# Low halves of an MLP's down weights: an adding DMA onto the negated high half, in place of a VectorE subtraction

## The chip, the cores and the metric

One core of a Trainium2 chip. The metric is the device time of one execution of the whole program in microseconds (us); lower is better. The kernel computes a forward pass on 512 tokens of width 1024, in float32.

## What is computed

The program runs a first block (two attentions, a memory cross-attention, a SwiGLU MLP) and then two layers of a second block, layer 0 (an mLSTM mixer) and layer 1 (latent attention). Both layers end in the MLP that the change touches, with w1 of 1024 x 4096 and w2 of 4096 x 1024:

```python
def sqrelu_mlp(h, w1, w2):
    return jnp.square(jax.nn.relu(h @ w1)) @ w2
...
    for l in range(DEPTH_2):
        ada = cond @ ada_w[l] + ada_b[l]
        sh1, sc1, g1, sh2, sc2, g2 = jnp.split(ada, 6, axis=-1)
...
        h = modulate(rmsnorm(x, norm_g[l, 2]), sh2, sc2)
        y = sqrelu_mlp(h, mlp_w1[l], mlp_w2[l])
        x = x + g2[:, None, :] * rmsnorm(y, norm_g[l, 3])
```

The products keep float32 accuracy: each operand is cut into a high part `hi`, the value rounded to the chip's short float32 form (fp32r), and a low part `lo = value - hi`. A product is then three matmuls: hi by hi, hi by lo, and lo by hi.

## The kernel before

**Weights.** Every weight matrix passes through one mechanism. `weights` (L410) declares *takes*: a take is a piece of a matrix of 512 KB, for a down matrix two k-tiles of 128 rows by 512 columns. `pump` loads the raw take with a DMA on SP's queue (L421) into one of four `raw` buffers, and calls `split` (L286), which allots one tile of the `s8` pool (14 buffers) for hi and lo together and appends the work in pieces. `plain` is a piece: ScalarE (ACT) copies the raw 128x512 to hi (L307), VectorE (DVE) subtracts hi from raw into lo (L308, where `f` is DVE here). In the stretches between two stages that the kernel calls quiet, every second hi is written by GpSimd (POOL, L304) in place of ACT. How many split takes may be held at once is the cap: 4, 3, 4, 4 and 4 in the five blocks of the MLP here (`caps`), and 7 while the last block's down products run. A raw buffer is free again when its last piece is done.

**The MLP.** `mlp` (L1322 on) goes over the 32 k-tiles of the hidden layer in blocks of 6, 8, 6, 6 and 6. For each block `up` makes the hidden tiles, squared ReLU and its split included, and the down products of that block add into eight accumulators. Block 0 comes from plain pairs of products (`relu_pairs`); blocks 1 to 4 from a Winograd form (`wino`): the product of quarters of w1 and h is made from seven smaller products, its matmuls of 256 columns are on L508, its combinations of PSUM results on DVE (L522 to L532), its weight sums in `split7` (ACT L341, DVE L342, L345, L361). The sums of h's quarters that it needs are made once by POOL (L480). Per layer the down products take 6, 8, 6, 6 and 6 takes, 32 in all; each feeds 24 matmuls of 512 columns (hi by hi on L445, hi by lo on L446, lo by hi on L447).

**Beside it.** During layer 0's MLP a background generator makes the rows `ada` of layer 1 and the shared keys: raw blocks of ada_w come in over SP's queue into `araw`, DVE multiplies and adds them up (L852), splits the sum (ACT L633, DVE L634), PE sums over the partitions (L869), DVE adds the bias row (L886). POOL issues the small DMAs around it (L201 for norm_g, ada_b and the store to `arow`; L585 reads rows back) and clears a tile for each row (L843). Layer 1's MLP has none of this beside it.

**Order.** The program is one stream per engine. A scheduler that simulates a timeline (`schedule_with_timeline_sim`) sets each engine's order when the kernel is built, so an edit can move instructions that it does not name. On each engine the instructions then run in order, and one that waits holds back all behind it. The raw loads are on SP's queue, the `ada` stores, row loads and small loads on POOL's.

Of the kernel before, what the change touches and what calls it, by code (L numbers as in the profile page):

```python
# [10 lines left out]
F32 = mybir.dt.float32  # L11
# [3 lines left out]
AF = mybir.ActivationFunctionType  # L15
ALU = mybir.AluOpType
# [5 lines left out]
S = 512  # L22
# [116 lines left out]
class Net:  # L139
# [64 lines left out]
    def pump(self):  # L204

        if self.dry:
            return
        more = True
        while more:
            more = False  # L210
            if self.n_load < len(self.specs):
                i = self.n_load
                kk, cc, loaders = self.specs[i][:3]
                if self.raw_live + len(loaders) <= BUF["raw"]:
                    self.raws[i] = [self.t("raw", [P, kk, cc], F32, BUF["raw"]) for _ in loaders]
                    for f in self.before.pop(i, ()):
                        f()
                    for loader, raw in zip(loaders, self.raws[i]):
                        loader(self, raw)
                    self.n_load += 1  # L220
                    self.raw_live += len(loaders)
                    more = True
            i, p = self.n_ready
            if i < self.n_load and self.w_live < self.wcap:
                kk, cc, loaders, gain = self.specs[i]
                if len(loaders) == 1:
                    self.ready[i, 0] = self.split(i, self.raws.pop(i)[0], kk, cc, gain)
                    self.n_ready = i + 1, 0
                else:
                    self.ready[i, p] = self.split7(i, p, self.raws[i])  # L230
                    self.n_ready = (i, p + 1) if p < 3 else (i + 1, 0)
                    if p == 3:
                        self.raws.pop(i)
                self.w_live += 1
                if not self.quiet and not BUF["sp"]:
                    while self.pieces:
                        _, last, f = self.pieces.pop(0)
                        f()
                        self.raw_live -= last
                more = True  # L240
# [13 lines left out]
            self.credit -= sp  # L254
            self.piece()

    def take(self, kk, cc, loader, gain=None):


        if self.dry:  # L260
            self.specs.append((kk, cc, loader, gain))
        self.n_take += 1
        return self.n_take - 1

# [18 lines left out]
            self.w_live -= 1  # L283
            self.pump()

    def split(self, c, src, kk, cc, gain):  # L286

        A, V = self.nc.scalar, self.nc.vector
        both = self.big([P, 2, kk, cc], F32R)
        hi, lo = both[:, 0], both[:, 1]  # L290
# [27 lines left out]
            V.scalar_tensor_tensor(out=lo[:, i, :], in0=src[:, i, :], scalar=g, in1=hi[:, i, :].bitcast(F32),  # L318
                                   op0=ALU.mult, op1=ALU.subtract)

        if gain is not None:
            todo = [lambda i=i: scaled(i) for i in range(kk)]
        else:
            m = min(cc, 512)
            todo = [lambda i=i, j=j: plain(slice(i, min(i + n, kk)), slice(j, j + m))
                    for i in range(0, kk, n) for j in range(0, cc, m)]
# [83 lines left out]
            self.step_bg()  # L410
        return self.gcols[name]

    def weights(self, w, k0, nk, c0, cn, view=None, gain=None, into=None):
        g = into or Group(self)
        kk = max(1, min(nk, 1024 // cn))
        for k in range(k0, k0 + nk, kk):
            n = min(kk, k0 + nk - k)

            def loader(net, raw, k=k, n=n):
                if view is None:  # L420
                    net.nc.sync.dma_start(out=raw, in_=w[k * P:(k + n) * P, c0:c0 + cn].rearrange(  # L421
                        "(k p) c -> p k c", p=P))
                else:
                    for i in range(n):
                        dst, src = view(raw[:, i, :], w[(k + i) * P:(k + i + 1) * P, :])
                        net.nc.sync.dma_start(out=dst, in_=src)

            g.add(self.take(n, cn, (loader,), gain and (gain, k)), n)
        return g

    def step_bg(self, n=1):
# [887 lines left out]
    def mlp(self, blocks, up, w_down, g, nxt, first, ready=None, caps=None):  # L1319
# [4 lines left out]
        for b, nb in enumerate(blocks):  # L1324
# [25 lines left out]

            if last:
                self.cap(BUF["lc"], True)
                wgs = [self.weights(w_down, k0, nb, c * S, S) for c in range(2)]

                def y_of(t):
                    ms = part(t, 0, product(t, wgs[0])) + part(t, 1, product(t, wgs[1]))
                    return acc[t], ms

                self.boundary(y_of, nxt, first)
            else:  # L1360
                for c in range(2):
                    wg = self.weights(w_down, k0, nb, c * S, S)
                    pss = [self.bank() for _ in range(NT)]
                    for k in range(0, nb, 2):
                        for t in range(NT):
                            self.run(self.prod(pss[t], [(hid.k(i, tt(t)), wg.k[i]) for i in (k, k + 1)],
                                               (lambda i: wg.used(k + i)) if t == NT - 1 else None,
                                               first=k == 0, last=k == nb - 2))
                    for t in range(NT):
                        part(t, c, pss[t])  # L1370
# [589 lines left out]
```

## Time and profile before

| | |
|---|---|
| median of 3 runs | 2034.83 us (2032.62 to 2037.33) |
| the profiled execution | 2033.3 us, span 2031.5 us, mean granted clock 0.982 |
| PE busy | 1941.8 us, 96 % of the span |
| DVE busy | 1396.7 us, 69 % |
| ACT busy | 1025.0 us, 50 % |
| POOL busy | 331.7 us, 16 %, 615 instructions |
| SP's DMA queue | 232.15 MB, 37.0 % of 16 engines |
| POOL's DMA queue | 11.10 MB, 1.9 % |
| chain that ended last | PE 69 %, DVE 14 %, issue 6 %, DMA 5 %, ACT 4 %, POOL 2 % |

The profiled execution took 2033.3 us by the clock of the runs, 1.8 us more than the span between its first and last instruction. Shares are means over stages that differ; the two MLPs in question lie at about 1100 to 1434 us (layer 0) and 1697 to 2024 us (layer 1). PE is TensorE, whose clock the chip throttles: 1.00 in the clock column is full speed.

### The profile page before, as it was taken

Reading aid. Unit: us, or ns where it says so; the run is one execution under the profiler, and the core shown is the slowest. Engines: PE = TensorE matmul, PEld = TensorE weight load, DVE = VectorE, ACT = ScalarE, POOL = GpSimd, SP = SyncE. Lnnn points to the kernel's source line nnn. Section 1 sums busy time; section 2 is a strip of 40 time slices with the busy share of each in tenths; the row PEclk is TensorE's granted clock in tenths of the full one; section 3 lists DMA queues with packets and bytes.
Section 4 is the critical chain, followed back from the end, with each engine's and each line's share of the span. In section 5 each row is a group of like instructions: output and inputs, shape, how many; then the busy total and the mean of one; then the engine's idle time right before and its main releaser. Section 6 shows DMA issues by size and latency. Waiting matters only on the chain.

```text
span 2031.5 us, 29708 instructions
## 1 busy us (share of the span) xinstructions
PE 1941.8 (96%) x10684; PEld 1665.1 (82%) x10684; DVE 1396.7 (69%) x2659; ACT 1025.0 (50%) x2283; POOL 331.7 (16%) x615
## 2 busy tenths in 40 slices
PE   8999998999999999999998899999979999999998
PEld 5888987778888888778888788798767978989987
DVE  5756645756576576757767897889758656657666
ACT  7767874545244233347534363454545644545444
POOL 1321113003000000421126100000330034000001
PEclk9999999999999999999999999999989999999999
DMA  7322341433465465244333355555342203233322
GB/s 219 89 79 76 118 129 61 137 104 103 157 202 159 137 203 142 83 142 129 120 104 113 117 163 156 183 167 159 102 134 89 73 12 103 83 104 115 103 74 83
DMA packets 191667, 245.14 MB, mean 121 GB/s; under 512 B 20059, under 2 KB 119488, under 8 KB 191520
## 3 DMA queue, kind: packets, MB, share of 16 engines
q1 hardware_dynamic: 185264, 232.15, 37.0%
q0 software_dynamic: 6256, 11.10, 1.9%
q8 instruction: 84, 1.38, 0.3%
q14 instruction: 63, 0.52, 0.1%
HBM read 241.00 MB, written 2.20 MB: 120 GB/s over the span
## 4 chain that ended last, share of the span: by engine, by line
PE 69%; DVE 14%; issue 6%; DMA 5%; ACT 4%; POOL 2%; DVEq 0%; POOLq 0%; ACTq 0%
PE ps L447 18%; PE ps L446 18%; PE ps L445 18%; PE ps L508 7%; DMA araw<-in_ada_w 3%; DVE u L852 2%; DVE s L308 2%; DVE s L318 2%; PE ps L1011 1%; DVE s L634 1%; DVE s L342 1%; DVE x L654 1%; ACT junk L579 1%; PE ps L1793 1%; PE ps L1822 1%
## 5 line engine op out<-in xcount | busy, mean ns | idle before, releaser
L445 PE MATMUL ps<-s,s 128*128 128x512 f32 (+4 forms) x2260 | 857.8, 383 | 8.4 <-ACT s L633 4.8
L446 PE MATMUL ps<-s,s 128*128 128x512 f32 (+4 forms) x2260 | 850.5, 377 | 12.2 <-DVE s L634 11.9
L447 PE MATMUL ps<-s,s 128*128 128x512 f32 (+4 forms) x2260 | 845.2, 377 | 4.7 <-DVE s L634 4.6
L446 PEld LDWEIGHTS ps<-s,s 128*128 128x128 f32 (+1 forms) x2260 | 431.7, 191 | 90.0 <-DVE s L634 13.7
L447 PEld LDWEIGHTS ps<-s,s 128*128 128x128 f32 (+1 forms) x2260 | 430.2, 190 | 86.7 <-DVE s L634 7.4
L445 PEld LDWEIGHTS ps<-s,s 128*128 128x128 f32 (+1 forms) x2260 | 429.7, 191 | 84.9 <-ACT s L633 7.5
L508 PE MATMUL ps<-s,s 128*128 128x256 f32 x2184 | 265.3, 282 | 10.0 <-DVE u L524 6.9
L508 PEld LDWEIGHTS ps<-s,s 128*128 128x128 f32 x2184 | 262.8, 189 | 13.8 <-issue 5.9
L852 DVE SCALAR_TENSOR_TENSOR u<-araw,cond,u 128x512 f32<-128x512 f32 x224 | 177.2, 791 | 108.6 <-DMA araw<-in_ada_w 87.2
L308 DVE TENSOR_TENSOR s<-raw,s 128x512 fp32r<-128x512 f32 x277 | 193.3, 736 | 42.5 <-ACT s L307 37.0
L307 ACT ACTIVATE s<-raw 128x512 fp32r<-128x512 f32 x255 | 144.9, 622 | 152.8 <-PE ps L447 96.4
L317 ACT ACTIVATE s<-raw,cols_all 128x256 fp32r<-128x256 f32 (+1 forms) x283 | 134.2, 547 | 47.5 <-issue 22.1
L318 DVE SCALAR_TENSOR_TENSOR s<-raw,cols_all,s 128x256 fp32r<-128x256 f32 (+1 forms) x305 | 150.5, 546 | 8.7 <-ACT s L317 7.3
L201 POOL DMA_DIRECT2D arow<-u x30 | 14.7, 492 | 629.6 <-DVE u L886 378.9
L568 POOL TENSOR_SCALAR sm<-sm 128x1 f32<-128x1 f32 x74 | 20.5, 277 | 558.9 <-ACT junk L579 556.1
L634 DVE TENSOR_TENSOR s<-ps,s 128x512 fp32r<-128x512 f32 (+3 forms) x124 | 75.2, 619 | 40.6 <-ACT s L633 39.7
L341 ACT ACTIVATE s<-raw 128x512 fp32r<-128x512 f32 x104 | 62.6, 621 | 67.9 <-PE ps L447 32.9
L634 DVE TENSOR_TENSOR s<-u,s 128x512 fp32r<-128x512 f32 x102 | 69.7, 686 | 39.4 <-ACT s L633 35.8
L633 ACT ACTIVATE s<-u 128x512 fp32r<-128x512 f32 x102 | 63.6, 625 | 64.0 <-DVE u L1403 49.3
L633 ACT ACTIVATE s<-ps 128x512 fp32r<-128x512 f32 (+3 forms) x124 | 65.2, 538 | 38.3 <-PE ps L626 16.1
L341 ACT ACTIVATE s<-u 128x512 fp32r<-128x512 f32 x78 | 48.7, 624 | 61.0 <-DVE u L345 31.6
L342 DVE TENSOR_TENSOR s<-raw,s 128x512 fp32r<-128x512 f32 x104 | 70.5, 682 | 11.0 <-ACT s L341 10.9
(264 smaller groups left out, 2211.7 us busy)
## 6 DMA issues: line engine op xcount, KB each, us to landing
raw<-in_mlp_w SPq DMA_DIRECT2D x128, 512.0 KB, 4.0
araw<-in_ada_w SPq DMA_DIRECT2D x192, 256.0 KB, 3.0
raw<-in_w_gate_up SPq DMA_DIRECT2D x44, 512.0 KB, 4.3
raw<-in_w_in SPq DMA_DIRECT2D x24, 512.0 KB, 4.6
raw<-in_a_w_in SPq DMA_DIRECT2D x24, 512.0 KB, 4.0
raw<-in_w_down SPq DMA_DIRECT2D x22, 512.0 KB, 4.1
raw<-in_w_mem_kv SPq DMA_DIRECT2D x16, 512.0 KB, 3.6
araw<-in_kv_ada_w SPq DMA_DIRECT2D x32, 256.0 KB, 3.1
```

The costliest lines, as they stand in the source:

```text
L307: A.activation(hi[:, sl, cl], src[:, sl, cl], AF.Copy)
L308: f.tensor_tensor(out=lo[:, sl, cl], in0=src[:, sl, cl], in1=hi[:, sl, cl].bitcast(F32), op=ALU.subtract)
L317: A.activation(hi[:, i, :], src[:, i, :], AF.Copy, scale=g)
L318: V.scalar_tensor_tensor(out=lo[:, i, :], in0=src[:, i, :], scalar=g, in1=hi[:, i, :].bitcast(F32), op0=ALU.mult, op1=ALU.subtract)
L341: A.activation(hi, x, AF.Copy)
L445: self.nc.tensor.matmul(ps, lhsT=ah, rhs=bh, start=first and i == 0, stop=False)
L446: self.nc.tensor.matmul(ps, lhsT=ah, rhs=bl, start=False, stop=False)
L447: self.nc.tensor.matmul(ps, lhsT=al, rhs=bh, start=False, stop=last and i == n - 1)
L508: nc.tensor.matmul(ps, lhsT=l[:, k, :], rhs=m[:, k, :], start=first and k == e == 0, stop=k == 3 and e == 2, skip_group_check=True)
L633: self.nc.scalar.activation(hi, x, AF.Copy)
L634: self.nc.vector.tensor_tensor(out=lo, in0=x, in1=hi.bitcast(F32), op=ALU.subtract)
L852: V.scalar_tensor_tensor(out=acc, in0=raws.pop(j - 2), scalar=vec[:, j - 2:j - 1], in1=acc, op0=ALU.mult, op1=ALU.add)
```

## The change

Takes can be marked `far`. The down takes of the squared-ReLU MLPs are (`caps` is set for these alone): 32 in each layer, 64 in all. For a far take, ACT writes hi as before, in two instructions, but within one piece; POOL then writes lo = -hi over the whole 128x1024, with a tensor_scalar (L326 of the changed kernel); and POOL issues a DMA that adds the raw take onto lo (L327), from SBUF to SBUF, 512 KB. So 128 subtractions leave DVE, 64 tensor_scalars and 64 DMAs come to POOL, and no far take's hi is made by POOL any more. The sums are the same. Lines behind the insertion stand 10 further down: L445, L446 and L447 become L455, L456 and L457, L508 becomes L518.

```diff
--- before.py
+++ after.py
@@ -222,9 +222,9 @@
                     more = True
             i, p = self.n_ready
             if i < self.n_load and self.w_live < self.wcap:
-                kk, cc, loaders, gain = self.specs[i]
+                kk, cc, loaders, gain, far = self.specs[i]
                 if len(loaders) == 1:
-                    self.ready[i, 0] = self.split(i, self.raws.pop(i)[0], kk, cc, gain)
+                    self.ready[i, 0] = self.split(i, self.raws.pop(i)[0], kk, cc, gain, far)
                     self.n_ready = i + 1, 0
                 else:
                     self.ready[i, p] = self.split7(i, p, self.raws[i])
@@ -254,11 +254,11 @@
             self.credit -= sp
             self.piece()
 
-    def take(self, kk, cc, loader, gain=None):
+    def take(self, kk, cc, loader, gain=None, far=False):
 
 
         if self.dry:
-            self.specs.append((kk, cc, loader, gain))
+            self.specs.append((kk, cc, loader, gain, far))
         self.n_take += 1
         return self.n_take - 1
 
@@ -283,7 +283,7 @@
             self.w_live -= 1
             self.pump()
 
-    def split(self, c, src, kk, cc, gain):
+    def split(self, c, src, kk, cc, gain, far=False):
 
         A, V = self.nc.scalar, self.nc.vector
         both = self.big([P, 2, kk, cc], F32R)
@@ -318,7 +318,17 @@
             V.scalar_tensor_tensor(out=lo[:, i, :], in0=src[:, i, :], scalar=g, in1=hi[:, i, :].bitcast(F32),
                                    op0=ALU.mult, op1=ALU.subtract)
 
-        if gain is not None:
+        def away():
+
+            G = self.nc.gpsimd
+            for i in range(0, kk, n):
+                A.activation(hi[:, i:i + n, :], src[:, i:i + n, :], AF.Copy)
+            G.tensor_scalar(out=lo, in0=hi.bitcast(F32), scalar1=-1.0, scalar2=1.0, op0=ALU.mult, op1=ALU.mult)
+            G.dma_start(out=lo, in_=src, accum_op=ALU.add)
+
+        if far:
+            todo = [away]
+        elif gain is not None:
             todo = [lambda i=i: scaled(i) for i in range(kk)]
         else:
             m = min(cc, 512)
@@ -410,7 +420,7 @@
             self.step_bg()
         return self.gcols[name]
 
-    def weights(self, w, k0, nk, c0, cn, view=None, gain=None, into=None):
+    def weights(self, w, k0, nk, c0, cn, view=None, gain=None, into=None, far=False):
         g = into or Group(self)
         kk = max(1, min(nk, 1024 // cn))
         for k in range(k0, k0 + nk, kk):
@@ -425,7 +435,7 @@
                         dst, src = view(raw[:, i, :], w[(k + i) * P:(k + i + 1) * P, :])
                         net.nc.sync.dma_start(out=dst, in_=src)
 
-            g.add(self.take(n, cn, (loader,), gain and (gain, k)), n)
+            g.add(self.take(n, cn, (loader,), gain and (gain, k), far), n)
         return g
 
     def step_bg(self, n=1):
@@ -1350,7 +1360,7 @@
 
             if last:
                 self.cap(BUF["lc"], True)
-                wgs = [self.weights(w_down, k0, nb, c * S, S) for c in range(2)]
+                wgs = [self.weights(w_down, k0, nb, c * S, S, far=caps is not None) for c in range(2)]
 
                 def y_of(t):
                     ms = part(t, 0, product(t, wgs[0])) + part(t, 1, product(t, wgs[1]))
@@ -1359,7 +1369,7 @@
                 self.boundary(y_of, nxt, first)
             else:
                 for c in range(2):
-                    wg = self.weights(w_down, k0, nb, c * S, S)
+                    wg = self.weights(w_down, k0, nb, c * S, S, far=caps is not None)
                     pss = [self.bank() for _ in range(NT)]
                     for k in range(0, nb, 2):
                         for t in range(NT):
```

**What moves.** On PE, at the start of layer 1's second block, nothing does. Here `s_3357` is the tile of the block's first down take, `s_3309` and `s_3310` hold the hidden tile's hi and lo. Before, from the last of the four L445 that open the block:

```order
L445 MATMUL ps_17758<-s_3357_17686,s_3309_17339 128x512
L508 MATMUL ps_17622<-s_3268_16975,s_3352_17651 128x256 [waits DVE_49]
L508 MATMUL ps_17622<-s_3268_16975,s_3352_17651 128x256 x9
L446 MATMUL ps_17755<-s_3357_17686,s_3309_17339 128x512 [waits DVE_49]
L447 MATMUL ps_17755<-s_3357_17686,s_3310_17340 128x512
L445 MATMUL ps_17755<-s_3357_17686,s_3309_17339 128x512 [waits Activation_49]
```

and with the change:

```order
L455 MATMUL ps_17758<-s_3357_17686,s_3309_17339 128x512
L518 MATMUL ps_17622<-s_3268_16975,s_3352_17651 128x256 [waits DVE_49]
L518 MATMUL ps_17622<-s_3268_16975,s_3352_17651 128x256 x9
L456 MATMUL ps_17755<-s_3357_17686,s_3309_17339 128x512 [waits DMASW1_49]
L457 MATMUL ps_17755<-s_3357_17686,s_3310_17340 128x512
L455 MATMUL ps_17755<-s_3357_17686,s_3309_17339 128x512 [waits Activation_49]
```

The matmuls stand in the same order, and the first one that reads lo waits for a DMA queue's semaphore in place of DVE's.

At the start of the third block of layer 1 PE's order is another (`s_3429` is the first down take, `s_3404` and `s_3405` hidden hi and lo; L508 rows are Winograd products of the next tiles). Before, again from the last of the four L445:

```order
L445 MATMUL ps_18437<-s_3429_18329,s_3404_18154 128x512
L446 MATMUL ps_18434<-s_3429_18329,s_3404_18154 128x512 [waits DVE_49]
L447 MATMUL ps_18434<-s_3429_18329,s_3405_18155 128x512
L445 MATMUL ps_18434<-s_3429_18329,s_3404_18154 128x512 [waits Activation_49]
L508 MATMUL ps_18297<-s_3184_16434,s_3418_18262 128x256 [waits Activation_49]
L508 MATMUL ps_18297<-s_3184_16434,s_3418_18262 128x256 x11
L446 MATMUL ps_18434<-s_3429_18329,s_3404_18154 128x512 [waits DVE_49]
L447 MATMUL ps_18434<-s_3429_18329,s_3405_18155 128x512
L446 MATMUL ps_18435<-s_3429_18329,s_3404_18154 128x512
L447 MATMUL ps_18435<-s_3429_18329,s_3405_18155 128x512
```

and with the change:

```order
L455 MATMUL ps_18437<-s_3429_18329,s_3404_18154 128x512
L518 MATMUL ps_18297<-s_3184_16434,s_3418_18262 128x256 [waits Activation_49]
L518 MATMUL ps_18297<-s_3184_16434,s_3418_18262 128x256
L518 MATMUL ps_18297<-s_3184_16434,s_3418_18262 128x256 [waits DVE_49]
L518 MATMUL ps_18297<-s_3184_16434,s_3418_18262 128x256 x9
L518 MATMUL ps_18298<-s_3232_16635,s_3418_18262 128x256 [waits DVE_49,Activation_49]
L518 MATMUL ps_18298<-s_3232_16635,s_3418_18262 128x256 x11
L518 MATMUL ps_18300<-s_3268_16975,s_3419_18281 128x256 [waits DVE_49]
L518 MATMUL ps_18300<-s_3268_16975,s_3419_18281 128x256 x11
L456 MATMUL ps_18434<-s_3429_18329,s_3404_18154 128x512 [waits DMASW1_49]
L457 MATMUL ps_18434<-s_3429_18329,s_3405_18155 128x512
```

The first hi by lo came right behind the four hi by hi; now 36 Winograd matmuls stand between them. The fourth and fifth blocks of layer 1 are ordered in this manner too.

On POOL, at the start of layer 0's MLP, before (`s_2070`, `s_2072`, `s_2074` are the first three down takes, `s_2106` the fourth; `u_2093` and on belong to the `ada` rows):

```order
L304 TENSOR_SCALAR s_2070_10684<-raw_10432 128x512 [waits DMAHW3_49,PE_49]
L304 TENSOR_SCALAR s_2072_10727<-raw_10507 128x512 [waits DMAHW4_49,PE_49]
L304 TENSOR_SCALAR s_2074_10746<-raw_10525 128x512 [waits DMAHW5_49,PE_49]
L585 DMA row_14375<-arow_4063 128x320 [waits DMASW1_49,DVE_49]
L201 DMA u_2093_10790<-in_kv_norm_g 1x16x32
L843 MEMSET u_2097_10836 128x512 [waits DMASW5_49]
L201 DMA u_2097_10836<-in_ada_b 1x16x32 [waits Pool_49]
L201 DMA arow_4063<-u_1934_9982 16x1x32 [waits DMASW2_49,DVE_49]
L381 DMA u_2094_10806<-arow_4063 8x128 [waits DMASW2_49]
```

and with the change:

```order
L326 TENSOR_SCALAR s_2070_10684<-s_2070_10684 128x1024 [waits PE_49,Activation_49]
L326 TENSOR_SCALAR s_2072_10727<-s_2072_10727 128x1024 [waits PE_49,Activation_49]
L327 DMA s_2070_10684<-raw_10432 128x1024 [waits DMAHW3_49,Pool_49]
L326 TENSOR_SCALAR s_2074_10746<-s_2074_10746 128x1024 [waits PE_49,Activation_49]
L327 DMA s_2072_10727<-raw_10507 128x1024 [waits DMAHW4_49,Pool_49]
L327 DMA s_2074_10746<-raw_10525 128x1024 [waits DMAHW5_49,DMASW2_49,Pool_49]
L326 TENSOR_SCALAR s_2106_10918<-s_2106_10918 128x1024 [waits PE_49,Activation_49]
L327 DMA s_2106_10918<-raw_10676 128x1024 [waits DMAHW6_49,Pool_49]
L201 DMA u_2093_10790<-in_kv_norm_g 1x16x32 [waits DMASW4_49]
L853 MEMSET u_2097_10836 128x512 [waits DMASW5_49]
L201 DMA u_2097_10836<-in_ada_b 1x16x32 [waits Pool_49]
L201 DMA arow_4063<-u_1934_9982 16x1x32 [waits DMASW6_49,DVE_49]
```

The negation and the adding DMA of four takes now stand ahead of the load of kv_norm_g and the clearing of the next `ada` row, and each such instruction waits for ACT's hi.

## Rows read from the trace of the kernel before

**Rows 1.** Windows of core 0: us, PE, PEld, DVE, ACT and POOL busy (instructions), clock, DMA share, GB/s.
```profile
1162.00:1429.00 267.00, 248.09 (x1577) 223.23 (x1576) 230.77 (x397) 129.43 (x243) 17.09 (x34) 0.98 0.54 166
1750.00:1995.00 245.00, 245.00 (x1596) 223.01 (x1595) 165.00 (x292) 126.36 (x238) 0.00 (x0) 1.00 0.32 101
```

**Rows 2.** Waits of PE from 1100 to 1434: total us, times, longest.
```profile
PE ps L869 <- DVE u L634: 10.6, 3, 5.2
PE ps L508 <- DVE u L524: 6.9, 3, 5.8
```

**Rows 3.** DVE by line, 1100 to 1434: busy us, mean ns | idle before.
```profile
L852 DVE SCALAR_TENSOR_TENSOR u<-araw,cond,u 128x512 f32<-128x512 f32 x80 | 69.5, 869 | 27.4 <-DMA araw<-in_ada_w 26.2 <-issue 0.6
L308 DVE TENSOR_TENSOR s<-raw,s 128x512 fp32r<-128x512 f32 x58 | 37.3, 683 | 1.6 <-ACT s L307 1.2
```

**Rows 4.** Timeline of PE: start, us, instruction; layer 1, second block.
```profile
1790.19 1.34 PE L508 MATMUL ps<-s,s 128*128 128x256 f32 x10
1791.37 0.39 PE L446 MATMUL ps<-s,s 128*128 128x512 f32 x1
```

**Rows 5.** Timeline of ACT: layer 1, second block.
```profile
1787.67 1.14 ACT L307 ACTIVATE s<-raw 128x512 fp32r<-128x512 f32 x2
...
1796.20 1.15 ACT L307 ACTIVATE s<-raw 128x512 fp32r<-128x512 f32 x2 [0.72 <-PE ps L447]
1801.76 1.15 ACT L307 ACTIVATE s<-raw 128x512 fp32r<-128x512 f32 x2 [4.41 <-PE ps L447]
```

**Rows 6.** POOL's line 304: ns min/median/max.
```profile
L304 POOL TENSOR_SCALAR s<-raw x22: 611/690/1081, 840.2 to 1690.3; 128x512 fp32r<-128x512 f32 x22
```

**Rows 7.** DMA issues: count, KB each, median us to landing.
```profile
row<-arow POOLq DMA_DIRECT2D x10, 512.0 KB, 4.3
...
u<-negc POOLq DMA_DIRECT2D x8, 256.0 KB, 3.7
...
row<-in_g_mix_post SPq DMA_DIRECT2D x1, 512.0 KB, 10.4
```

**Rows 8.** Windows around two long waits of PE in layer 0.
```profile
1284.00:1288.00 4.00, 1.08 (x3) 0.89 (x4) 3.94 (x9) 1.66 (x4) 1.01 (x2) 0.89 0.77 282
1288.00:1292.00 4.00, 4.00 (x13) 3.16 (x13) 3.96 (x7) 0.00 (x0) 1.06 (x3) 0.68 0.72 236
...
1424.00:1428.00 4.00, 2.22 (x10) 2.25 (x11) 3.94 (x8) 0.61 (x2) 0.00 (x0) 0.50 0.81 287
1428.00:1432.00 4.00, 4.00 (x16) 3.31 (x15) 1.89 (x5) 2.70 (x5) 0.49 (x1) 0.69 0.49 138
```

**Rows 9.** Timeline of PE: these two waits.
```profile
1286.91 0.63 PE L869 MATMUL ps<-u,onesr 128*128 128x512 f32 x1 [4.15 <-DVE u L634]
...
1425.78 2.90 PE L508 MATMUL ps<-s,s 128*128 128x256 f32 x12 [5.77 <-DVE u L524]
```

**Rows 10.** Timeline of ACT: layer 1, third block.
```profile
1856.17 1.14 ACT L307 ACTIVATE s<-raw 128x512 fp32r<-128x512 f32 x2
```

**Rows 11.** Timeline of PE: layer 1, third block.
```profile
1860.29 1.10 PE L445 MATMUL ps<-s,s 128*128 128x512 f32 x4
```

**Rows 12.** Timeline of POOL: layer 0, first block.
```profile
1096.56 0.52 POOL L201 DMA_DIRECT2D u<-in_kv_norm_g  x1
...
1112.17 0.49 POOL L201 DMA_DIRECT2D arow<-u  x1 [13.75 <-DVE u L886]
```

**Rows 13.** Timeline of ACT: layer 0, first and second block.
```profile
1106.42 1.14 ACT L307 ACTIVATE s<-raw 128x512 fp32r<-128x512 f32 x2
...
1205.83 1.14 ACT L307 ACTIVATE s<-raw 128x512 fp32r<-128x512 f32 x2
```

**Rows 14.** Timeline of PE: layer 0, second block.
```profile
1206.50 1.19 PE L445 MATMUL ps<-s,s 128*128 128x512 f32 x4 [2.77 <-ACT s L307]
```

**Rows 15.** Timeline of DVE: layer 0, beside POOL's products.
```profile
1113.78 12.19 DVE L852 SCALAR_TENSOR_TENSOR u<-araw,cond,u 128x512 f32<-128x512 f32 x3
```

**Rows 16.** Timeline of POOL: the same stretch.
```profile
1114.55 10.07 POOL L480 TENSOR_TENSOR u<-s 128x512 f32<-128x512 f32 x8
```

## The prediction

> **What bounds the kernel now.** I read first the windows of the two MLPs, from the first Winograd product of each to its last [rows 1]. In layer 1 PE is busy 245.00 of 245 us at clock 1.00, with DVE at 165 us: nothing but matmuls sets the time there, and an edit that shortens no matmul can only lose. In layer 0 the same work takes 267 us, with PE busy 248.09, clock 0.98 and DVE busy 230.77, that is 86 %. So 22 us are there to be had, at most, and the list of PE's waits [rows 2] says from whom: 10.6 us for the sums of `ada` that DVE splits, 6.9 us for DVE's additions that free a PSUM bank. Both are an engine late with its queue. DVE's lines of this stretch [rows 3] show what fills it: `ada` 69.5 us, and the subtraction L308 with 58 instructions of 683 ns. L308 is what the change takes away, in both layers.
>
> **Where lo is needed.** In the middle of a block the change has room: ACT starts a take's hi when PE has finished an older take, at 1796.20 and 1801.76 us [rows 5], and that take is used two takes later, some 11.1 us. At the start of a block there is none: ACT writes hi while PE is at the last Winograd products. In layer 1's second block hi is there at 1787.67 + 1.14 = 1788.81 us [rows 5], and the first matmul that reads lo ran at 1791.37, after ten small ones of 0.118 us each [rows 4]. That is 2.6 us later, enough for two subtractions, and the order of PE there is unchanged.
>
> **The cost of a far lo.** The trace of before has neither a 128x1024 tensor_scalar on POOL nor an adding DMA.
> - L326: the nearest row is POOL's 128x512 tensor_scalar, 0.61 to 1.08 us, median 0.69 [rows 6]. Twice that: 1.4 us taken, 1.2 to 2.2 as ends.
> - L327: issue to landing on POOL's queue is 3.7 us for 256 KB and 4.3 for 512 KB [rows 7], so 0.6 us for each 256 KB on a base of 3.1. An add must fetch what stands in lo besides raw, so I count the bytes twice: 3.1 + 2 x 1.2 = 5.5 us taken. The low end is 3.7, the quickest of POOL's two rows; the high end 10.4, the slowest landing of 512 KB [rows 7].
> Together 6.9 us from hi to lo, where the subtraction took 0.7. ACT's work stays as it was and costs nothing. In mid-block 1.14 + 6.9 = 8.0 us lie within the 11.1, so those takes, with their 128 fewer subtractions, cost layer 1 nothing; their cover is gone when an add needs more than 8.6 us.
>
> **Part by part, against the profiled 2033.3 us.**
> - *Layer 1, second block.* Lo is there at 1788.81 + 6.9 = 1795.7, wanted at 1791.4: PE waits 4.3 us (1788.81 + 1.2 + 3.7 gives 2.3, 1788.81 + 2.2 + 10.4 gives 10.0). What an idle PE pays besides is seen in layer 0: a wait of 4.15 us at 1286.91 [rows 9] was followed by windows at 0.89 and 0.68 [rows 8], hence 4 x (0.11 + 0.32) = 1.7 us, between the two levels of 2.4 and 1.2 GHz. **+6.0.**
> - *Layer 1, third to fifth block.* Here the scheduler moved 36 Winograd matmuls ahead of the first reader of lo. In the third, hi ends at 1856.17 + 1.14 = 1857.31 [rows 10], lo is there at 1864.2, and the reader comes after the four L445 from 1860.29, 1.0 us, and 36 x 0.118 = 4.2 us, at 1865.5 [rows 4, 11]. Covered by 1.3 us; the other two alike. **0**, or up to 5 us each at the slow end.
> - *Layer 0, POOL's order.* The load of kv_norm_g ran at 1096.56 and the store of a finished `ada` row waited for DVE until 1112.17 [rows 12]. Now four negations and adds stand ahead of the load, the fourth not before its hi at 1106.42 + 1.14 [rows 13]: 1107.6 + 1.4 + 0.5 for its issue, and 0.5 + 0.6 + 0.3 + 0.5 us of POOL instructions, is 1111.4, just before the store. +1 (0 to 4). Further on the adds of takes five and six stand behind another store that waits for DVE: +1 (0 to 5). **+2.**
> - *Layer 0, second block.* Hi ends at 1206.97 [rows 13], lo is there at 1213.9. PE's order now has 24 Winograd matmuls after the four L445 at 1206.50 [rows 14], so the reader is due at 1206.5 + 1.0 + 2.8 = 1210.3. **+3.6** (1.6 to 9.3). The third block starts behind the `ada` wait of 1286.91, the fourth has 36 matmuls for cover, the fifth starts late behind the 5.77 us wait: 0 (up to 3 each).
> - *The added traffic.* 32 adds of 512 KB in layer 0, read twice and written once, beside 166 GB/s in 267 us [rows 1]. DVE already sits 26.2 us waiting for `araw` [rows 3]. **+3** (0 to 10).
> - *DVE's relief in layer 0.* 64 subtractions of about 0.64 us each, as they stand back to back, are 41 us less [rows 3]. But POOL and DVE get in each other's way: three L852 took 12.19 us [rows 15] while POOL ran eight two-input products of 10.07 us [rows 16]; three at their mean of 869 ns would be 2.6. If the tensor_scalars L326 hold DVE up as those products did, 32 x 1.4 = 45 us come back as waits of DVE; if not at all, 41 us stay gained. I take a good half blocked, some 18 us net, a twelfth of DVE's load, and let that shorten the waits of [rows 9] by two fifths: **-4** (0 to -15).
>
> The Trainium skill speaks against the change here ("SBUF — State Buffer", the section on the shared port pair): a VectorE instruction with two SBUF inputs and a GpSimd instruction that reads SBUF exclude each other, and the second waits until the first is done. The trace agrees for GpSimd products [rows 15, 16]; for a tensor_scalar no row here settles it. By that rule in full the relief would be nil and the sum 4 us higher.
>
> Sum: 6.0 + 0 + 2 + 3.6 + 3 - 4 = +10.6, so 2033.3 + 10.6 = **2043.9, say 2044 us**. The profiled run is 1.5 us below the median of the three shown, so against the median it is +9 to +10.
>
> **Rivals.**
> - *Slower by more: the adds land late.* If an add takes 8 us or more (between 5.5 and 10.4), the layer 1 stall is 1788.81 + 1.4 + 8 - 1791.37 = 6.8 plus 2 for the clock, the three other blocks there lose 1.2 each, layer 0's second block 6.1 and two others some 4 each, and POOL's order 4 to 5; mid-block is just still covered. With traffic 3 and no relief: 6.8 + 2 + 3.6 + 6.1 + 8 + 4.5 + 3 = +34, 2067 us, or 2062 with the traffic hidden and one block covered. For it: one queue carries all adds, and small loads share it. Against: POOL's queue is nearly empty now and its rows are at 4.3.
> - *Faster: DVE is relieved.* Where POOL's tensor_scalar does not block DVE, 41 us go from 231. The two waits of [rows 9] go, 4.15 + 5.77, with their clock: 1.7 and, from 1424 on, 4 x (0.50 + 0.31) = 3.2 [rows 8]; -14.8 in all. It decides if besides an add lands as the 512 KB loads do, in 4.3 us: layer 1's wait is then 1788.81 + 1.2 + 4.3 - 1791.37 = 2.9 (so short a wait I cost at no clock), layer 0's second block 1206.97 + 5.5 - 1210.3 = 2.2. Sum -9.7, 2023.6 us. For it: in layer 0 DVE is what PE waits for. Against: POOL's products held DVE up for 10 us [rows 15, 16], and layer 1 has nothing to give.
> - *No change.* Relief in layer 0 of some 8 us against the 6 of layer 1 and 2 to 3 at layer 0's block starts: 2030 to 2038.
>
> **How the numbers follow.** About 0.2 %, 4 us, can be told from no change. Forecast, slower by 5 to 20 us: 0.40. Late adds: 0.12. No change: 0.18. Faster: 0.30. Slower in all 0.52. The forecast's own range, with its terms' ends, is 2038 to 2054. The range asked for takes in the faster rival with some us below and the late adds: 2020 to 2066.
>
> **What would show it.** In the changed profile: a wait of PE on the first hi by lo (L456) of layer 1's second block, for a DMA, of 4 us, and none in the next three; PE busy short of the stretch by that much in layer 1's window; L326 at about 1.4 us, L327 at 5.5 from issue to landing; DVE in layer 0's window below 215 us, with single two-input instructions of DVE well over 0.75 us where L326 runs. I am wrong if layer 1 has no wait, if adds land in 4 us or in 10, or if layer 0's window shrinks by over 10 us.

## The result, and the profile after

The changed kernel took 2082.44 us, median of 4 runs (2076.28 to 2084.86), beside 2033.72 for the kernel before: ratio 1.0236, 95 % interval 1.0205 to 1.0268. By the ratio that is 48 us slower, where 10 were forecast and the range ended at 2066.

Where it went is read first from windows laid at the same work as [rows 1], from the first Winograd product to the last of either MLP (columns as there), and one over the whole MLP of layer 0.

```profile
1183.00:1463.00 280.00, 250.32 (x1560) 224.72 (x1558) 208.24 (x342) 126.72 (x238) 65.94 (x80) 0.97 0.68 191
1788.00:2034.00 246.00, 242.07 (x1575) 220.53 (x1574) 137.94 (x241) 122.72 (x232) 45.88 (x47) 0.99 0.56 141
1095.00:1475.00 380.00, 330.22 (x1998) 294.62 (x1997) 266.16 (x410) 163.05 (x303) 109.44 (x114) 0.94 0.65 178
```

The kernel before, over the whole MLP of layer 0:

```profile
1095.00:1440.00 345.00, 320.23 (x1981) 285.91 (x1980) 289.72 (x475) 162.52 (x302) 33.29 (x53) 0.98 0.51 157
```

DVE did get its time back (266 us in place of 290), and PE still took 35 us longer. By these rows 25 of them are idle time of PE (380 - 330.22 = 49.8 us in place of 345 - 320.23 = 24.8). The other 10 are longer busy time for the same matmuls, beside a granted clock of 0.94 in place of 0.98: behind the wait that ended at 1170.18 us the clock was 0.50 and a matmul of 512 columns took 0.63 us, where it takes 0.39 at 1.00. PE's waits after, 1095 to 1475 us, beside [rows 2] (L879 is L869 of before, L518 is L508, L395 the transpose of a finished `ada` row):

```profile
PE ps L456 <- DMA s<-raw: 15.0, 2, 8.7
PE ps L879 <- DVE u L644: 12.9, 4, 7.4
PE ps L518 <- DVE u L534: 8.1, 5, 3.9
PE ps L395 <- DMA u<-arow: 5.8, 2, 3.1
PE ps L518 <- DVE u L536: 5.0, 2, 3.3
```

Two waits for lo are new, and so are those for the `arow` load; the waits for DVE that its relief should have shortened are longer in total than before, and DVE itself waits longer. Its `ada` line in the same stretch, beside [rows 3]:

```profile
L862 DVE SCALAR_TENSOR_TENSOR u<-araw,cond,u 128x512 f32<-128x512 f32 x80 | 72.6, 908 | 64.8 <-DMA araw<-in_ada_w 64.2
```

27.4 us idle before it have become 64.8, nearly all for the loads of ada_w. In layer 1 PE waited for lo three times, 6.1 us in all.

### The profile page after: what moved, and what is told of

Its sections match the earlier page's. It is cut to its first block, busy times and chain, and to the rows that moved or that the text cites. A ratio compares the mean times of both kernels' runs of the same rounds, so it can differ in the third digit from the quotient of the medians.

```text
span 2079.4 us, 29848 instructions
## 1 busy us (share of the span) xinstructions
PE 1956.5 (94%) x10684; PEld 1676.1 (81%) x10684; DVE 1344.7 (65%) x2531; ACT 1026.8 (49%) x2288; POOL 467.4 (22%) x738
## 3 DMA queue, kind: packets, MB, share of 16 engines
q1 hardware_dynamic: 185264, 232.15, 35.6%
## 5 line engine op out<-in xcount | busy, mean ns | idle before, releaser
L456 PE MATMUL ps<-s,s 128*128 128x512 f32 (+4 forms) x2260 | 854.3, 379 | 31.0 <-DMA s<-raw 21.1
L455 PE MATMUL ps<-s,s 128*128 128x512 f32 (+4 forms) x2260 | 854.0, 384 | 8.3 <-ACT s L643 6.4
L457 PE MATMUL ps<-s,s 128*128 128x512 f32 (+4 forms) x2260 | 850.8, 379 | 5.0 <-DVE s L644 4.8
L456 PEld LDWEIGHTS ps<-s,s 128*128 128x128 f32 (+1 forms) x2260 | 433.3, 192 | 109.5 <-DMA s<-raw 22.8
L457 PEld LDWEIGHTS ps<-s,s 128*128 128x128 f32 (+1 forms) x2260 | 432.3, 191 | 87.6 <-DVE s L644 7.6
L455 PEld LDWEIGHTS ps<-s,s 128*128 128x128 f32 (+1 forms) x2260 | 430.9, 191 | 85.3 <-ACT s L643 9.0
L518 PE MATMUL ps<-s,s 128*128 128x256 f32 x2184 | 269.8, 285 | 14.5 <-DVE u L534 8.1
L518 PEld LDWEIGHTS ps<-s,s 128*128 128x128 f32 x2184 | 266.8, 193 | 18.1 <-ACT u L538 5.7
L326 POOL TENSOR_SCALAR s<-s 128x1024 fp32r<-128x1024 f32 x64 | 89.3, 1402 | 351.9 <-ACT s L325 284.5
L317 ACT ACTIVATE s<-raw,cols_all 128x256 fp32r<-128x256 f32 (+1 forms) x283 | 134.0, 547 | 47.0 <-issue 18.8
L308 DVE TENSOR_TENSOR s<-raw,s 128x512 fp32r<-128x512 f32 x149 | 110.1, 774 | 20.8 <-ACT s L307 15.3
L644 DVE TENSOR_TENSOR s<-u,s 128x512 fp32r<-128x512 f32 x102 | 84.2, 832 | 54.9 <-ACT s L643 51.3
L351 ACT ACTIVATE s<-u 128x512 fp32r<-128x512 f32 x78 | 48.8, 625 | 76.4 <-DVE u L355 45.7
L1353 DVE TENSOR_TENSOR u<-ps,u 128x512 f32<-128x512 f32 x80 | 53.5, 683 | 49.1 <-PE ps L457 48.9
```

What stands on the lines that cost most here:

```text
L308: f.tensor_tensor(out=lo[:, sl, cl], in0=src[:, sl, cl], in1=hi[:, sl, cl].bitcast(F32), op=ALU.subtract)
L317: A.activation(hi[:, i, :], src[:, i, :], AF.Copy, scale=g)
L326: G.tensor_scalar(out=lo, in0=hi.bitcast(F32), scalar1=-1.0, scalar2=1.0, op0=ALU.mult, op1=ALU.mult)
L351: A.activation(hi, x, AF.Copy)
L455: self.nc.tensor.matmul(ps, lhsT=ah, rhs=bh, start=first and i == 0, stop=False)
L456: self.nc.tensor.matmul(ps, lhsT=ah, rhs=bl, start=False, stop=False)
```

## Experiments

Ratios are to the kernel before, on the same chip; "position" is how much later than in the kernel before PE reached a point, in the profiled executions, which differ by a few us from run to run: that of e_l1only was its slowest (2049.73 us), and stands at +7.0 before layer 1, where it has no far take yet.

The expectations weigh four theories of the loss. A: POOL's negation and DVE hold each other up. B: the adds hold the `raw` buffers longer, so the loads behind them on SP's queue come later. C: the adds' traffic on the DMA engines, and lo that comes late. D: POOL's queue runs in order, and its small loads stand behind the adds. Most edits also change the order that the scheduler sets on PE, DVE and ACT, so that a difference between two runs is that of the edit together with its order. One pair is free of this, e_memcopy and e_nowait: in their traces PE, DVE, ACT and POOL run the same instructions in the same order.

| | ratio (95 %) | first Winograd matmul, layer 0 | last, layer 0 | first, layer 1 | last matmul |
|---|---|---|---|---|---|
| the change | 1.0236 (1.0205 to 1.0268) | +20.3 | +34.0 | +37.2 | +45.7 |
| e_l1only | 1.0031 (1.0014 to 1.0048) | +2.7 | +5.9 | +7.0 | +16.4 |
| e_notfirst | 1.0125 (1.010 to 1.015) | +13.4 | +24.0 | +22.6 | +23.9 |
| e_actneg | 1.0198 (1.0165 to 1.023) | +2.6 | +27.6 | +34.9 | +42.3 |
| e_nolo | 0.9925 (0.9903 to 0.9947) | +1.5 | -8.3 | -13.0 | -13.2 |
| e_memcopy | 0.9951 (0.9931 to 0.9971) | +2.2 | -9.2 | -7.8 | -7.9 |
| e_nowait | 1.0122 (1.0081 to 1.0163) | +6.7 | +18.5 | +20.0 | +21.7 |

**Which layer, and which takes.** Two edits of the flag:

```diff
-...far=caps is not None...                  # e_l1only, parts of lines
+...far=self.far_now...                      # set for layer 1's MLP alone
-...gain and (gain, k), far), n)             # e_notfirst
+...gain and (gain, k), far and (c0 > 0 or k > k0)), n)
```

`e_l1only`, expected:

> Far takes in layer 1's MLP alone (32 in place of 64). If layer 0 is where most of the 48 us went, layer 1 by itself costs what its stretch of the changed kernel shows, some 9 to 11 us: about 2043 us. By the prediction's own term for layer 1 (+6) about 2040. If the loss were spread evenly over the 64 takes: about 2058.

Measured 2043.12 us, as expected for the first case, ratio 1.0031: layer 1 costs 6 us by the ratio, 9.4 by positions (from +7.0 to +16.4). Some 40 of the 48 us lie in layer 0.

`e_notfirst`, expected:

> The change, but the first down take of each block is split the old way (10 of 64 takes). The prediction's term for layer 1 (the wait at the second block's start, with its clock) is gone: layer 1 costs 4 us or less in place of some 10. Were lo's latency at block starts the main loss in layer 0 as well, the whole would fall to 2040 to 2055; by theory B, where every take holds raw, it stays at 2062 or more.

Measured 2062.88 us. In layer 1 the position moves by 1.3 us only: there the loss was the first takes of the blocks, as forecast. PE's waits of this run from 1680 us on show one left for lo:

```profile
PE ps L456 <- DMA s<-raw: 0.8, 1, 0.8
```

In layer 0 the first takes are worth 15 us (+22.6 at the start of layer 1, in place of +37.2), and 22 remain, so lo's lateness at block starts is not the main loss there. The whole lies where theory B had put it.

**The port that POOL and DVE share.** The fifth take of layer 0, in the changed kernel, on POOL's timeline:

```profile
1151.45 12.50 POOL L326 TENSOR_SCALAR s<-s 128x1024 fp32r<-128x1024 f32 x1 [15.84 <-ACT s L325]
```

and DVE's timeline of the same stretch:

```profile
1151.84 0.67 DVE L644 TENSOR_TENSOR s<-u,s 128x512 fp32r<-128x512 f32 x1
1152.43 0.67 DVE L493 TENSOR_TENSOR u<-u,u 128x512 f32<-128x512 f32 x1
1153.04 0.73 DVE L862 SCALAR_TENSOR_TENSOR u<-araw,cond,u 128x512 f32<-128x512 f32 x1
...
1162.37 0.67 DVE L352 TENSOR_TENSOR s<-u,s 128x512 fp32r<-128x512 f32 x1
1163.08 1.41 DVE L371 SCALAR_TENSOR_TENSOR u<-u,raw 128x512 f32<-128x512 f32 x1
```

A negation of 1.06 us (the median of 64) took 12.50. It began at 1151.45, and DVE, which had no gap between its two-input instructions, ran them at 0.67 to 0.73 us each right through it; POOL ended at 1163.95, inside the first DVE instruction that is longer, 1.41 us. PE got this lo at 1170.18, after its longest wait, 8.7 us. Other runs that keep the negations have a long one at the same place: 9.42 us in e_notfirst, 4.03 in e_raw6s13, 3.31 in e_dveadd.

```diff
-            G.tensor_scalar(out=lo, in0=hi.bitcast(F32), scalar1=-1.0, scalar2=1.0, op0=ALU.mult, op1=ALU.mult)  # e_actneg
+            for i in range(0, kk, n):
+                A.activation(lo[:, i:i + n, :], src[:, i:i + n, :], AF.Copy, scale=-1.0)
-            G.dma_start(out=lo, in_=src, accum_op=ALU.add)                   # e_dveadd
+            for i in range(0, kk, n):
+                V.tensor_tensor(out=lo[:, i:i + n, :], in0=lo[:, i:i + n, :].bitcast(F32), in1=src[:, i:i + n, :], op=ALU.add)
```

`e_actneg`, expected:

> ACT writes the negated high half from raw (scale -1), GpSimd only issues the adding DMA. Theory A (GpSimd and VectorE exclude each other, GpSimd's negation starves under VectorE's two-input runs and slows them): the 12.5 us negation is gone, DVE's two-input instructions are back at 0.68 us, layer 0 gives back 20 us or more, 2045 to 2062 us. Theory B (the adding DMA reads raw late, so the four raw buffers are held some 7 us longer per take and SP's in-order queue brings Winograd and ada loads later): only the one long negation's share, under 12 us, comes back, 2070 us or more. Theory C (only the latency of lo at block starts and the added traffic): 2075 or more.

Measured 2077.62 us, 8 us below the change by the ratios, which theories B and C allow and A does not. The first Winograd product comes 17.7 us earlier than in the change, as theory A has it, and by layer 1 all but 2.3 us of it are lost again to other waits: theory A is right for that place and wrong for the sum.

`e_dveadd`, expected:

> GpSimd negates as in the change, but VectorE adds raw (two 128x512 each take) in place of the DMA. Theory A: as many two-input VectorE instructions as in the kernel before against GpSimd's 64 negations, long negations stay or get longer, 2060 or more. Theory B: no DMA holds raw, loss small, 2035 to 2050. Theory C: lo is 1 us later than before at block starts only, about 2038.

Measured 2044.90 us, ratio 1.0045 (1.003 to 1.0059). With POOL's negations kept, and no DMA, 9 us are lost in place of 48. Theory A falls as the main cause; the time lies within theory B's range and 7 us above theory C's figure, so B seemed right.

**The held raw buffers.** In the change SP waited 86 us for adds to release raw in layer 0 (it had waited 68 for L308). Three ways to take that away, and a control:

```diff
-            G.dma_start(out=lo, in_=src, accum_op=ALU.add)                   # e_hbm
+            G.dma_start(out=lo, in_=far(), accum_op=ALU.add)                 # far(): the rows of w in HBM
-            G.tensor_scalar(out=lo, in0=hi.bitcast(F32), scalar1=-1.0, scalar2=1.0, op0=ALU.mult, op1=ALU.mult)  # e_hold
-            G.dma_start(out=lo, in_=src, accum_op=ALU.add)
+            for i in range(0, kk, n):
+                V.scalar_tensor_tensor(out=lo[:, i:i + n, :], in0=hi[:, i:i + n, :].bitcast(F32), scalar=-2.0,
+                                       in1=src[:, i:i + n, :], op0=ALU.mult, op1=ALU.add)
+            G.dma_start(out=lo, in_=hi.bitcast(F32), accum_op=ALU.add)
-BUF = dict(s8=14, u2=16, row=3, raw=4, ...                                   # e_raw6s13, b_raw6s13
+BUF = dict(s8=13, u2=16, row=3, raw=6, ...
```

`e_hbm`, expected:

> The adding DMA takes its source from the weight matrix in HBM in place of the raw tile, GpSimd still negates: raw is free as soon as ACT has read it. Theory B: raw loads wait less than in the kernel before, layer 0's loss falls to about 10 us and the total to 2045 to 2060. Theory A: GpSimd's long negations stay, 2070 or more. Theory C: latency as before or longer and 33.5 MB more read from HBM, 2080 or more.

Measured 2095.27 us, ratio 1.0296 (1.0257 to 1.0335): slower than the change; an add took 9.1 us to land, in place of 6.4.

`e_hold`, expected:

> VectorE writes raw - 2*hi as lo (two 128x512 scalar_tensor_tensor each take) and the adding DMA adds hi, from the same tile: as many adding DMAs, bytes and waits for lo as in the change, but raw is free as soon as VectorE has read it, and GpSimd computes nothing. Theory B (the held raw buffers): layer 0 loses at most 15 us, in all 2045 to 2058. Theory C (the adds' traffic slows the other loads, and lo is late at block starts): layer 0 loses 25 us or more, 2062 or more. VectorE's relief is gone here, which weighs on both alike.

Measured 2090.29 us, 1.0254 (1.0223 to 1.0285).

`e_raw6s13`, expected:

> The change with six raw buffers in place of four (and 13 split tiles in place of 14, for room). Theory B: two more buffers cover the longer hold, the distance to the control below falls from 48 to 25 us or less. Theory C: it stays at 40 or more.

`b_raw6s13`, expected:

> Control: the kernel before with six raw buffers and 13 split tiles. Within 10 us of the kernel before by both theories.

Measured 2103.98 and 2043.07 us (1.0332, 1.0305 to 1.0358, and 1.0032, 1.0017 to 1.0048): the distance between the two grew to 61 us. Theory B predicted the other side in all three, where theory C's ranges hold, and B falls as the main cause. That the hold costs nothing isn't shown: the adds of e_hbm and e_hold also landed later than the change's (median 9.1 and 8.6 us in place of 6.4), and each of these runs has another order.

**What the adds cost when nobody reads them.** Here the matmuls read hi in lo's place: these kernels leave the low halves out of their products, and lo's lateness with them.

```diff
-        return hi, lo                                       # all of this group
+        return hi, (hi if far else lo)
-            G.tensor_scalar(out=lo, in0=hi.bitcast(F32), scalar1=-1.0, scalar2=1.0, op0=ALU.mult, op1=ALU.mult)
-            G.dma_start(out=lo, in_=src, accum_op=ALU.add)  # e_nolo: nothing in their place
+            G.memset(lo.bitcast(F32), 0.0)                  # e_nowait, e_nowaithi, e_memcopy
+            G.dma_start(out=lo, in_=src, accum_op=ALU.add)  # e_nowait; e_nowaithi: in_=hi.bitcast(F32)
+            G.dma_start(out=lo.bitcast(F32), in_=src)       # e_memcopy, e_copypool; e_copyact: A.dma_start
```

`e_nolo`, expected:

> Leaves out the low half of the 64 far takes altogether: ACT writes hi, the matmuls read hi in lo's place; no negation, no DMA, no subtraction. This is the most that VectorE's relief can give. If the prediction's rival (VectorE relieved, its two waits in layer 0 and their clock gone) is right about the size: 2015 to 2024. If layer 0's waits come from the order of the loads rather than from VectorE's load: 2028 to 2036.

Measured 2019.48 us, 0.9925: DVE's relief, with no lo to wait for, is worth 15 us, as the rival "faster" had worked out (-14.8). That the two agree so closely is luck: the rival has all of it in layer 0's stretch, where the positions show 10 us (from +1.5 to -8.3), with 5 more between the layers.

`e_nowait`, expected:

> As before this one, but GpSimd clears lo (a memset, which reads no SBUF) and the adding DMA adds raw onto it, as in the change; nobody reads lo, the matmuls read hi. Traffic, raw hold and GpSimd's queue as in the change; lo's lateness and the negation's port lock are gone. If the loss is lo's lateness (port lock, landing, block starts) with the clock it costs: 2040 or less. If it is traffic, hold or GpSimd's queue: 2055 or more.

Measured 2058.25 us. Positions: +20.0 at the start of layer 1, +21.7 at its end. So adds whose result PE does not read cost next to nothing in layer 1, and in layer 0 33 us against e_nolo (+20.0 and -13.0).

`e_nowaithi`, expected:

> As the last, but the DMA adds hi in place of raw, so raw is free after ACT. Its distance below the last is the price of the held raw buffers: theory B 15 us or more, theory C 5 or less.

Measured 2073.56 us (1.0205), 15 us more with raw freed early, where theory B had 15 less. The adds landed later here (median 9.6 us, 7.6 in e_nowait) and DVE, ACT and POOL run in another order, so this does not give the price of the hold.

`e_copypool`, expected:

> Low halves left out as in the run of that kind (matmuls read hi); GpSimd's queue issues a plain 512 KB copy from raw to lo for each far take in place of clearing and adding, nobody reads it. Same places in GpSimd's order, same hold of raw, but the DMA engines move the bytes once without fetching lo. Theory C (traffic on the DMA engines; an add occupied them 2.9 us each against 1.6 for a load): about half of the 39 us that the unread adds cost falls away, 2030 to 2045. Theory D (GpSimd's in-order queue: the small ada DMAs stand behind DMAs that wait for ACT and raw): 2050 or more.

`e_copyact`, expected:

> The same unread copy, issued on ACT's queue: GpSimd's order is that of the run with the low halves left out. Theory C: within 6 us of the copy on GpSimd's queue. Theory D: near the run with the low halves left out, 2028 or less.

Measured 2029.94 (0.9976, 0.9963 to 0.9988) and 2029.15 us (0.9963, 0.9949 to 0.9978). Against e_nolo moving the bytes costs 8 to 10 us, and whose queue issues them makes no difference that can be told: theory D falls. Theory C held but for its size: of the 39 us that the unread adds cost, 28 fall away, not half.

`e_memcopy`, expected:

> Low halves left out (matmuls read hi); GpSimd clears lo and then issues a plain 512 KB copy from raw onto it, nobody reads it: GpSimd's order, its memsets and the hold of raw are those of the run with unread adds, and the one difference is that the DMA copies where that one adds. Theory C (the add's own work on the DMA engines): near the unread copies, 2025 to 2036. Theory D (GpSimd's memsets and order): near the unread adds, 2050 or more.

Measured 2026.61 us. All four compute engines run in e_nowait's order, and the one difference is that the DMA copies where that one adds. 35 us hang on it by the ratios (0.9951 against 1.0122, whose intervals allow 22 to 47), 30 by the positions. POOL's DMA queue on the page of e_memcopy (kind: packets, MB, share of 16 engines' span):

```profile
q0 software_dynamic: 15472, 44.66, 6.4%
```

and on that of e_nowait:

```profile
q0 software_dynamic: 15472, 44.66, 10.9%
```

The same packets and bytes, and without any (e_nolo) the queue has 2.0 %. So the packets of 64 copies took the 16 engines 6.4 % x 2025.8 - 2.0 % x 2018.4 = 89 us, 1.4 us each; those of 64 adds 10.9 % x 2055.4 - 40 = 184 us, 2.9 us each. A load of 512 KB in the kernel before: 37.0 % of 2031.5 us for 232.15 MB, 1.7 us. What that did to others is seen at the `ada` loads of layer 0's MLP. From issue to landing, in e_memcopy:

```profile
DMA to landing us min/median/max: 2.2/3.1/7.3
```

and in e_nowait:

```profile
DMA to landing us min/median/max: 2.3/3.4/9.9
```

DVE's line that waits for them (columns as in [rows 3]), in e_memcopy:

```profile
L862 DVE SCALAR_TENSOR_TENSOR u<-araw,cond,u 128x512 f32<-128x512 f32 x80 | 68.7, 859 | 49.8 <-DMA araw<-in_ada_w 46.0 <-DMA u<-in_ada_b 3.3
```

and in e_nowait:

```profile
L862 DVE SCALAR_TENSOR_TENSOR u<-araw,cond,u 128x512 f32<-128x512 f32 x80 | 69.7, 872 | 65.8 <-DMA araw<-in_ada_w 57.3 <-DMA u<-in_ada_b 7.8
```

The median hardly moves, and the longest says little by itself (7.8 us in e_nolo, without any added transfer). The late ones become more: of the 58 `ada` loads with a known landing 17 took over 5 us in e_nowait, 7 in e_memcopy, and 3 of 60 in e_nolo. DVE idles 16 us more, and PE's waits for `ada` (L879) go from 7.6 us in two to 15.6 in four, with 6.3 for L395. The windows (columns as in [rows 1]) show what this comes to for PE, in e_memcopy:

```profile
1085.00:1430.00 345.00, 326.18 (x2045) 293.17 (x2045) 257.64 (x417) 167.79 (x314) 86.52 (x124) 0.97 0.62 205
```

and in e_nowait:

```profile
1085.00:1460.00 375.00, 338.29 (x2055) 302.60 (x2054) 258.31 (x417) 167.69 (x313) 97.84 (x124) 0.94 0.67 186
```

PE idles 36.7 us in place of 18.8, and is busy 12 us longer at the lower clock. But the same pair also differs in the hold of the raw buffers. SP's waits before its loads (L431) for an add or copy to release raw, in e_memcopy:

```profile
SPq L431 <- DMA s<-raw: 22.5, 10, 5.6
```

and in e_nowait:

```profile
SPq L431 <- DMA s<-raw: 42.0, 13, 8.8
```

With those of the other raw loads (L504, 18.0 and 21.3 us) SP waits 23 us more. So theory B is alive as a part of the 35 us: the add's slower landing can delay the next loads, beside what its traffic does to the loads under way.

**Two other forms.** e_best puts e_actneg's edit and e_notfirst's together, with the flag set for layer 0's MLP alone; e_pooltt has one GpSimd instruction in place of negation and DMA:

```diff
-            G.tensor_scalar(out=lo, in0=hi.bitcast(F32), scalar1=-1.0, scalar2=1.0, op0=ALU.mult, op1=ALU.mult)
-            G.dma_start(out=lo, in_=src, accum_op=ALU.add)
+            G.tensor_tensor(out=lo, in0=src, in1=hi.bitcast(F32), op=ALU.subtract)
```

`e_best`, expected:

> Layer 0 alone, ACT writes the negated half, and the first down take of each block is split the old way: 27 far takes. Port lock (about 18 us to the first Winograd product) and late first takes are both out; what is left is traffic, hold and GpSimd's queue. If those are small: 2030 to 2040, near or below the kernel before; if they carry the rest of what the run without first takes lost in layer 0: 2045 to 2055.

Measured 2057.24 us, 1.0118 (1.0076 to 1.0159), 2 us above the higher of the two ranges, with 27 adds, all in layer 0: the first Winograd product at +2.5, then +26 at layer 1. The parts don't add up to a kernel that gains.

`e_pooltt`, expected:

> No DMA: GpSimd itself subtracts hi from raw (one tensor_tensor of 128x1024 each far take). VectorE is relieved as in the change and no traffic is added. If traffic is the main loss: near or below the kernel before, 2025 to 2040, less what the two-input GpSimd instruction (some 2.5 us each) costs VectorE by the port. If the port lock decides: 2045 or more.

Measured 2064.93 us, 1.0146 (1.0118 to 1.0174), 45 us more than e_nolo without any added traffic. POOL's instruction takes 2.42 us (median), and DVE's `ada` line, from 1085 to 1472 us, 1042 ns in place of 869 [rows 3]:

```profile
L861 DVE SCALAR_TENSOR_TENSOR u<-araw,cond,u 128x512 f32<-128x512 f32 x80 | 83.3, 1042 | 34.1 <-DMA araw<-in_ada_w 30.4 <-DMA u<-in_ada_b 3.1
```

DVE was busy for 311 us of this stretch, where e_nolo's (1085 to 1430) has 260 with about as many instructions. That is what the expectation had from the port lock; the order differs as well, and no run here holds it fixed.

## Why the prediction failed

By the ratios, on 2034 us: the relief -15 (e_nolo), the copies with POOL's memset +5 (e_memcopy), adding in place of copying +35 (e_nowait), and from there to the change, with lo read by PE and the negation in place of the memset, +23; they make +48 by construction. Each is good to some us, and all but the +35 hold a change of order too. The prediction had the sign, and these steps:

- *Layer 1, second block, +6.0*: right. ACT's hi ended at 1825.82, the add was issued at 1827.27, and PE waited:

```profile
1827.19 1.34 PE L518 MATMUL ps<-s,s 128*128 128x256 f32 x10
1832.46 0.79 PE L456 MATMUL ps<-s,s 128*128 128x512 f32 x1 [3.93 <-DMA s<-raw]
```

  3.93 us beside 4.3 forecast, matmuls at 0.63 us in place of 0.39 behind it, and the position from +37.0 to +43.5 at the next block. It landed 5.2 us after its issue; 5.5 was taken.
- *Third to fifth block, 0*: right but for two waits of 1 us in the last block.
- *Layer 0, POOL's order, +2, at most 9*: too small. By the first Winograd product 20.3 us were lost. The load of kv_norm_g went out at 1115.11 us, where 1109.5 follows from the working, since the fourth negation began at 1113.20 only; and PE waited 3.1 us for `arow` there, which is new. But most of it is the long negation of the fifth take: without negations on POOL (e_actneg) the place stands at +2.6.
- *L326, 1.4 us, 1.2 to 2.2*: wrong in its upper end. The median is 1.06, but one took 12.50. The prediction priced the port in one direction only, as DVE's waits for POOL. Here POOL waited for DVE. The rule that it cited from the Trainium skill ("SBUF — State Buffer", "Summary: rules for kernel authors": the second of the two to issue is blocked until the first is done) names no side; the trace agrees with it in this direction too, over a run of DVE instructions rather than one (12.50 us).
- *Layer 0, second block, +3.6*: the wait was 6.35 us, within the bounds; its add went out at 1226.74, 7.7 us before PE could go on (5.5 was taken).
- *The added traffic, +3, at most 10*: this is the step that failed. The add's bytes were counted twice for its own landing, and the engines' time bears that out (2.9 us for 1.4), but the price for everybody else was a guess, set beside 166 GB/s and DVE's 26.2 us of waits for `araw`. Unread, the adds cost 5 us as copies and 35 more as adds. Late then are the `ada` loads, POOL's small ones, and the raw loads whose buffers the adds hold, on chains that PE waits for.
- *DVE's relief, -4*: it is worth -15 with the low halves left out, the rival's figure. The change never gets it: DVE idles 64.8 us before its `ada` line in place of 27.4.
- *The clock* was counted for one wait. PE has thirteen of more than 1.2 us in layer 0's MLP, in place of six, and was busy 10 us longer there.
- *The range of the forecast, "2038 to 2054, with its terms' ends"*: the ends that the terms state add up to -11 and +62, so 2022 to 2096. Had they been added, 2082 would have lain inside; the narrower range is that of "slower by 5 to 20 us".

The rival "late adds" (2062 to 2067 us) came nearest, with the same underpriced traffic. In part that is luck: it wanted landings of 8 us or more, and the median is 6.4 (6.8 in layer 0, up to 10.6).

Left open: how much of the 35 us is the engines' occupancy, how much the longer hold of raw (7.6 us to landing for an unread add, 4.5 for a copy) and how much the longer issue on POOL (0.87 us and 0.53) was not separated. Why adding hi in place of raw is slower still is not explained either; hi and lo lie in one tile and such adds landed in 9.6 us, in place of 7.6, but the order differs too. No version here beats the kernel before and computes the low halves.

## What to carry to other kernels

Price a moved operation by what it takes from the resource that it moves to, and ask who else's late arrival PE pays for: here some 41 us of VectorE, by the prediction's estimate, went to DMA engines that already carried the stage's critical loads. A run that leaves the work out altogether shows about how much any move can win (15 us here), and an unread copy and an unread add then price the move before the latency is looked at. Where a scheduler may reorder the program, look for a pair of runs whose order is the same: its difference is the edit's alone. Where a stage waits for scattered late landings, medians say little; count the late ones, and count each wait with the clock that follows it.

## What the runs showed that was not expected

The packets of an adding DMA of 512 KB within SBUF took the 16 engines 2.9 us, those of a plain copy of the same bytes 1.4 us. A GpSimd tensor_scalar that reads SBUF took 12.50 us in place of 1.06, as long as a gapless run of VectorE two-input instructions went on. And two more raw buffers (with one split tile fewer, and another order) made the kernel with adds some 20 us slower, the kernel without them 7.
